# A decoder-plus-mixture kernel: expert weights in 8 KB runs, a twentieth buffer, and the overflow branch at the program's end

## The chip, the cores and the metric

The kernel runs on one core of one Trainium2 chip. The metric is the device time of one execution in microseconds (us), the median of repeated runs. Traces come from one profiled execution.

## The reference, cut to what matters

Two blocks run one after the other on 256 tokens of width 1024, all in fp32. The first block has two layers (feed-forward, retention and differential attention, feed-forward). The second block has one layer with a mixer and then a mixture of experts, and the change lies in the mixture.

```python
g_logits = h @ w_grp + b_grp                  # 4 groups
grp = argmax(g_logits)                        # one group per token
top_val, top_idx = top_k(e_logits[grp], 2)    # two of its 8 experts
gate = softmax(top_val) * p_grp
# per expert e, on the tokens that chose it:
out = (silu(xb @ w1[e]) * (xb @ w3[e])) @ w2[e]   # w1, w3: 1024x512, w2: 512x1024
y = sum of gate * out over a token's two experts
x = x + g2 * y
```

There are 32 experts. Their three matrices hold 6 MB per expert and 192 MB in all, and every one is read once from device memory.

## The kernel before, in words

The experts are worked on in 16 pairs (`pairs`, loop over `g`, NPAIR = 16). Each expert of a pair has 64 slots (CAP), so that a pair fills the 128 rows of the array's output. A pair's steps on TensorE stand in a fixed order, because every matmul of this part goes through `pin`, which keeps program order:

- `first`: 64 recorded matmuls `ph`, the tokens times w1 (bank ph0) and w3 (bank ph1), 128x64 weights against 512 columns; ScalarE puts the Silu of ph0 into `h`, VectorE multiplies ph1 in.
- `tokens(nxt)`: the gather for the next pair. For each of eight chunks k of the width, two matmuls of the normed tokens `h2` with the 0/1 matrix `pick` fill a bank `xgp`; it is scaled and shifted into `xg`, by ScalarE where k is even and by VectorE where it is odd. The banks are `tp` and `po` by turns.
- `turned`: four transposes of h into bank `ot`; `turned_out` copies one half with ScalarE, the other with VectorE into `hTe`.
- `combine(prev)`: the previous pair's weighted rows `yh` and `yl` go back to the tokens (`po` matmuls) and VectorE adds them to `xtok`. It comes in two halves of 512 columns, one ahead of each half of `last`.
- `last`: `py`, h times w2, 512 output columns at a time. After each half `weighed` makes `y` (VectorE), `yh` (ScalarE) and `yl` (VectorE).
- `slots(nxt)`: transposes and gates of the next pair, between the halves of `last`.

`route` comes before the pairs: it computes the logits, the choice of experts, each token's place in its expert and the gates.

Weights come in pieces of 1 MB into 19 places of 1 MB (`ring`), twelve pieces for a pair, all issued by SyncE's queue (SP) in order of use. A piece waits for its place, and a place becomes free when the matmuls of the piece that it held are done. Most places are memory of the mixer that ends just before (tiles such as hT, sA, xhi, raw), and the last two (e0, e1, MW = 2) belong to the mixture alone. A piece of w1 or w3 is loaded with rows k*128+p on partition p, so that its runs in device memory are one row, 512 floats or 2 KB. A piece of w2 takes half a row, 2 KB too:

```python
dma_start(w[:, k0:k1, a:b], ap[row + k0 * P:row + k1 * P, col + a:col + b]
          .rearrange("(k p) f -> p k f", p=P))
```

If an expert has more than 64 tokens, a branch (`overflow`, a `tc.If` with a loop over all pairs in it) works on the rest. With these inputs it isn't taken. It stands between pair 6 and pair 7 (OVERFLOW = 7). There the pipeline is emptied first: pair 6 is combined at once, every engine loads the largest count (`mi`) and compares and branches, and pair 7 starts after it. Pair 7's loads are issued ahead of the branch. The last pair has its pieces and its w2 product in smaller cuts, and sends each quarter of the output off as it is done.

Of the kernel before, what the change touches and what calls it, by code (L numbers as in the profile page):

```python
# [147 lines left out]
CUTS = {True: ((0, 256, 512), (0, 256, 512)), False: ((0, 512), (0, 512))}  # L148
ORD = (((0, 1, 6, 7),), ((2, 3), (4,), (5,)))
OVERFLOW = 7  # L150
MW = 2
# [15 lines left out]
def _pf_layout():  # L167
    o = 0
    for name, n in (("f1n0", 8), ("f1n1", 8), ("mxn0", 8), ("mxn1", 8), ("f2n0", 8), ("f2n1", 8),
                    ("fin", 8), ("n1w", 8), ("gn0", 4), ("gn1", 4), ("sub0", 1), ("sub1", 1),  # L170
                    ("c", 8), ("cctx", 8), ("hgw", 1), ("n2w", 8)):
# [8 lines left out]
class Kernel:  # L180
# [633 lines left out]
    def modulation(self):  # L814
# [7 lines left out]
        self.m2col = self.cp.tile([P, 2, KC], F32, name="m2col")  # L822
        self.mrow = self.dp.tile([8, 1, D], F32, name="mrow")
        for part in range(6):
# [17 lines left out]
            for i in range(1 + both):  # L842
# [17 lines left out]
                nc.scalar.dma_start(mrow, row)  # L860
                if part not in (2, 5):
                    nc.scalar.dma_start(self.mcol[:, 2 * i + part] if both else self.m2col[:, part - 3],
                                        mrow.rearrange("o (k p) -> p (o k)", p=P))
# [11 lines left out]
        nc.vector.scalar_tensor_tensor(self.rc, self.rc, 1.0, self.pf[:, o:o + KC], op0=ALU.add, op1=ALU.mult)  # L875
        cst = self.cp.tile([P, 64 + 36 + P], F32, name="cst")
# [610 lines left out]
    def pairs(self):  # L1487
# [9 lines left out]
        for g in range(NPAIR):  # L1497
            if 0 < g < OVERFLOW or g > OVERFLOW:
                ws = self.loads(g)
# [7 lines left out]
            h = self.late.tile([P, 512], F32, name="h", tag="h", bufs=1)  # L1507
            self.nc.scalar.activation(h, ph, AF.Silu)
# [3 lines left out]
            self.nc.vector.tensor_tensor(h, h, ph, op=ALU.mult)  # L1512
# [13 lines left out]
            elif g:  # L1526
                self.outputs(cur)
            if g < end:
                self.last(py, hT, ws[4], cur, 0, slice(0, 512))
                if due:  # L1530
                    self.combine(prev, due.pop(0))
                flush = g + 1 == OVERFLOW
                if not flush:
                    self.slots(nxt, self.gate_te[:, :, 2 * g + 2:2 * g + 4])
                self.last(py, hT, ws[5], cur, 1, slice(0, 512))
                prev = cur
                if flush:
                    for n in range(2):
                        self.combine(prev, slice(512 * n, 512 * n + 512))
                    ws = self.loads(g + 1)  # L1540
                    self.overflow()
                    prev = None
# [3 lines left out]
            for n in range(2):  # L1546
                for c in (slice(a, b) for a, b in zip(CUTS[True][n], CUTS[True][n][1:])):
                    self.last(py, hT, ws[4 + n], cur, n, c)
# [3 lines left out]
            self.combine(cur, due.pop(0), True)  # L1552

# [3 lines left out]


# [332 lines left out]
```

## Time and profile before

| | |
|---|---|
| median of 3 runs | 1817.65 us (1817.04 to 1818.62) |
| profiled execution, its own time | 1815.69 us |
| its span, first to last instruction | 1814.0 us |
| mean granted TensorE clock | 0.99 |
| busy share of the span: TensorE, VectorE, ScalarE, GpSimd | 97%, 57%, 41%, 19% |
| read from device memory | 424.56 MB |

The sums below are made in the span of the profiled execution; its own time is 1.7 us longer than the span and 2.0 us below the median. The experts take the last 500 us. Everything before 1300 us belongs to the first block and the mixer. DMA share is the mean busy share of the core's 16 DMA engines; packets of one engine overlap a little, so that a full load reads 1.05.

### The profile page before, as it was taken

To read this page: it belongs to the slowest core of one execution; us is meant where nothing else is said; L and a number is where in the kernel's file an instruction comes from. 1 tells how busy PE (TensorE), PEld (TensorE's weight loads), DVE (VectorE), ACT (ScalarE), POOL (GpSimd) and SP (SyncE) were. 2 spreads that over 40 slices of the span, in tenths; PEclk is the share of its full clock that TensorE was granted. 3 is DMA by queue.
4 is the path that set the end of the run, shared out by engine and by line. 5 is a ranking of instruction groups with operands and counts; after the bars stand their busy time and mean duration, and the time that the engine had idled before them with its cause. 6 is when DMAs were issued, how large, how long until landed. Compare 5 with 4: busy or idle time off the path is not lost. (4 is left out here: it accounts for less than half of the span.)

```text
span 1814.0 us, 30657 instructions
## 1 busy us (share of the span) xinstructions
PE 1757.8 (97%) x12435; PEld 1439.5 (79%) x12435; DVE 1035.4 (57%) x1764; ACT 737.1 (41%) x1312; POOL 343.8 (19%) x341
## 2 busy tenths in 40 slices
PE   9999999999999999999999999999989999899998
PEld 8999988899999999999899999986654444344444
DVE  6875887676667667668677755648332323122323
ACT  6444445454444544444455544656421111111111
POOL 3231273121221213236131102311000000000000
PEclk9999999999999999999999999999989999899999
DMA  8766643255677576754355655431789999999998
GB/s 253 231 209 192 227 163 117 70 171 166 206 232 247 174 249 211 232 189 133 114 172 170 187 190 164 160 123 41 248 315 380 397 400 400 397 400 400 399 398 306
DMA packets 312946, 427.75 MB, mean 236 GB/s; under 512 B 15056, under 2 KB 207312, under 8 KB 312672
## 3 DMA queue, kind: packets, MB, share of 16 engines
q1 hardware_dynamic: 294640, 394.51, 63.1%
q10 hardware_dynamic: 18160, 31.23, 5.2%
q8 instruction: 100, 1.64, 0.4%
q14 instruction: 46, 0.38, 0.1%
HBM read 424.56 MB, written 1.15 MB: 235 GB/s over the span
## 5 line engine op out<-in xcount | busy, mean ns | idle before, releaser
L265 DVE TENSOR_TENSOR whl<-raw,whl 128x1024 fp32r<-128x1024 f32 (+2 forms) x374 | 464.4, 1246 | 208.5 <-ACT whl L264 207.5
L264 ACT ACTIVATE whl<-raw 128x1024 fp32r<-128x1024 f32 (+2 forms) x374 | 383.8, 1032 | 331.2 <-PE pd L275 107.9
L273 PE MATMUL pgu<-xh,whl 128*128 128x272 f32 (+1 forms) x1408 | 403.8, 287 | 3.6 <-DVE g L348 3.3
L275 PE MATMUL pgu<-xh,whl 128*128 128x272 f32 (+1 forms) x1408 | 403.1, 286 | 2.4 <-DVE whl L265 2.4
L274 PE MATMUL pgu<-xl,whl 128*128 128x272 f32 (+1 forms) x1408 | 402.9, 286 | 1.4 <-DVE xl L286 1.4
L273 PEld LDWEIGHTS pgu<-xh,whl 128*128 128x128 f32 x1408 | 264.1, 188 | 5.5 <-issue 3.5
L275 PEld LDWEIGHTS pgu<-xh,whl 128*128 128x128 f32 x1408 | 265.0, 188 | 3.2 <-DVE whl L265 3.0
L274 PEld LDWEIGHTS pgu<-xl,whl 128*128 128x128 f32 x1408 | 265.1, 188 | 2.3 <-DVE xl L286 2.0
L1767 PE MATMUL ph<-ew,xg 128*64 128x512 f32 x1024 | 225.4, 597 | 6.8 <-issue 6.8
L275 PE MATMUL pd<-ah,whl 128*128 128x272 f32 (+1 forms) x704 | 203.2, 289 | 0.3 <-DVE whl L265 0.3
L274 PE MATMUL pd<-al,whl 128*128 128x272 f32 (+1 forms) x704 | 202.4, 288 | 0.0
L273 PE MATMUL pd<-ah,whl 128*128 128x272 f32 (+1 forms) x704 | 202.3, 287 | 0.0
L1767 PEld LDWEIGHTS ph<-ew,xg 128*64 128x64 f32 x1024 | 74.1, 138 | 152.0 <-issue 148.3
L352 POOL TENSOR_TENSOR u<-u,g 128x272 f32<-128x272 f32 (+1 forms) x88 | 92.1, 1047 | 397.1 <-DVE u L351 339.9
L273 PEld LDWEIGHTS pd<-ah,whl 128*128 128x128 f32 x704 | 132.9, 189 | 0.5 <-issue 0.2
L273 PE MATMUL pj<-xh,whl 128*128 128x272 f32 x448 | 133.2, 298 | 0.0
L275 PEld LDWEIGHTS pd<-ah,whl 128*128 128x128 f32 x704 | 132.5, 188 | 0.6 <-DVE whl L265 0.5
L274 PEld LDWEIGHTS pd<-al,whl 128*128 128x128 f32 x704 | 132.8, 189 | 0.1
L274 PE MATMUL pj<-xl,whl 128*128 128x272 f32 x448 | 130.5, 291 | 0.5 <-DVE xl L286 0.5
L275 PE MATMUL pj<-xh,whl 128*128 128x272 f32 x448 | 130.1, 290 | 0.0
L1787 PE MATMUL py<-ew,hTe 128*64 128x512 f32 (+1 forms) x544 | 117.4, 573 | 2.1 <-ACT hTe L1779 1.0
L1512 DVE TENSOR_TENSOR h<-h,ph 128x512 f32<-128x512 f32 x16 | 11.0, 687 | 175.6 <-PE ph L1767 175.6
(442 smaller groups left out, 2733.2 us busy)
## 6 DMA issues: line engine op xcount, KB each, us to landing
ew<-in_w_dram SPq DMA_DIRECT2D x180, 1024.0 KB, 13.8
raw<-in_ffn_w_gate_dram SPq DMA_DIRECT2D x43, 1024.0 KB, 5.5
raw<-in_ffn_w_up_dram SPq DMA_DIRECT2D x43, 1024.0 KB, 5.6
raw<-in_w_in_dram SPq DMA_DIRECT2D x38, 1024.0 KB, 5.1
raw<-in_ffn_w_down_dram SPq DMA_DIRECT2D x32, 1024.0 KB, 6.2
mraw<-in_w_mod_dram ACTq DMA_DIRECT2D x24, 1024.0 KB, 6.0
raw<-in_ffn_w_down_dram SPq DMA_DIRECT2D x16, 768.0 KB, 5.4
ew<-in_w_dram SPq DMA_DIRECT2D x24, 512.0 KB, 11.0
```

What stands on the lines that cost most here:

```text
L264: nc.scalar.activation(w[:, 0], part, AF.Copy)
L265: nc.vector.tensor_tensor(w[:, 1], part, w[:, 0].bitcast(F32), op=ALU.subtract)
L273: nc.tensor.matmul(out, wh, xh, start=first, stop=False)
L274: nc.tensor.matmul(out, wh, xl, start=False, stop=False)
L275: nc.tensor.matmul(out, wl, xh, start=False, stop=last)
L352: nc.gpsimd.tensor_tensor(u[:, :N], u[:, :N], g[:, :N], op=ALU.mult)
L1512: self.nc.vector.tensor_tensor(h, h, ph, op=ALU.mult)
L1767: self.pin(self.nc.tensor.matmul(ps[hj], cur["xg"][:, 4 * kk + k, hj], w[j][:, k], start=kk + k == 0, stop=kk == 1 and k == 3))
L1787: self.pin(self.nc.tensor.matmul(py[hj, n, c], hT[:, k, hj], w[j][:, k, c], start=k == 0, stop=k == 3))
```

## The change

- The rows of w1, w3 and w2 are dealt to the partitions in blocks: partition p holds rows 8p to 8p+7 of w1 and w3 and rows 4p to 4p+3 of w2. A piece then takes four neighbouring rows of 2 KB (w1, w3) or two neighbouring rows of 4 KB (w2), which is one run of 8 KB per partition. Pieces stay 1 MB. Only the last pair keeps smaller cuts.
- A piece of w2 is now half of its rows over all 1024 columns, not all rows over half of the columns. So `last` works through rows, and both halves of `weighed` come after its second part. The last pair uses `last_part`, which is the former order.
- The other dealing of rows is matched on the chip: h2 is written in another order of its columns, `h` is written and read with a stride of four, and scale and shift of the gather come from a second copy (`rce`, `she`), for which the mixture's modulation loads two more small rows (`m2e`).
- The gather puts odd chunks into the three rotating banks `mm` and even chunks into `tp` and `po` by turns, four or five banks where there were two.
- A twentieth place (e2, MW = 3). Its memory comes from tiles that now share or lose a buffer: `pick` and `xg` have one instead of two, `y` shares `h`, the router's small tiles share `yh`, `yl`, `hTe`.
- The branch is the last part of the program, behind the output's transfers, without the hint on which side falls through. Its own loads go to SP's queue instead of GpSimd's, and it sends the output again when it is taken. The pipeline isn't emptied between pairs 6 and 7.

```diff
@@ -145,10 +145,9 @@
 NPAIR = 16
 CAP = 64
 
-CUTS = {True: ((0, 256, 512), (0, 256, 512)), False: ((0, 512), (0, 512))}
+CUTS = ((0, 256, 512), (0, 256, 512))
 ORD = (((0, 1, 6, 7),), ((2, 3), (4,), (5,)))
-OVERFLOW = 7
-MW = 2
+MW = 3
 CONSTS = [
...
+                    nc.scalar.dma_start(self.m2e[:, part - 3], mrow.rearrange("o (p k) -> p (o k)", p=P))
...
+        self.she, self.rce = self.m2e[:, 0], self.m2e[:, 1]
+        o = PF["n2e"][0]
+        nc.vector.scalar_tensor_tensor(self.rce, self.rce, 1.0, self.pf[:, o:o + KC], op0=ALU.add, op1=ALU.mult)
...
-            if 0 < g < OVERFLOW or g > OVERFLOW:
+            if g:
...
@@ -1504,12 +1510,12 @@
             self.first(ph, cur, ws[1], 1)
             if not prev:
                 self.slots(cur, self.gate_te[:, :, 2 * g:2 * g + 2])
-            h = self.late.tile([P, 512], F32, name="h", tag="h", bufs=1)
-            self.nc.scalar.activation(h, ph, AF.Silu)
+            h = self.late.tile([P, 4, P], F32, name="h", tag="h", bufs=1)
+            self.nc.scalar.activation(self.by_row(h), ph, AF.Silu)
             ph = self.mm("ph1")
             for kk in range(2):
                 self.first(ph, cur, ws[2 + kk], kk)
-            self.nc.vector.tensor_tensor(h, h, ph, op=ALU.mult)
+            self.nc.vector.tensor_tensor(h, h, ph.rearrange("p (q k) -> p k q", k=4), op=ALU.mult)
...
             if prev:
                 cur["yh"], cur["yl"] = prev["yh"], prev["yl"]
-            elif g:
-                self.outputs(cur)
             if g < end:
-                self.last(py, hT, ws[4], cur, 0, slice(0, 512))
+                self.last(py, hT, ws[4], 0)
                 if due:
                     self.combine(prev, due.pop(0))
-                flush = g + 1 == OVERFLOW
-                if not flush:
-                    self.slots(nxt, self.gate_te[:, :, 2 * g + 2:2 * g + 4])
-                self.last(py, hT, ws[5], cur, 1, slice(0, 512))
+                self.slots(nxt, self.gate_te[:, :, 2 * g + 2:2 * g + 4])
+                self.last(py, hT, ws[5], 1)
+                for n in range(2):
+                    self.weighed(py, cur, n, slice(0, 512))
                 prev = cur
-                if flush:
-                    for n in range(2):
-                        self.combine(prev, slice(512 * n, 512 * n + 512))
-                    ws = self.loads(g + 1)
-                    self.overflow()
-                    prev = None
                 cur = nxt
                 continue
             due = []
             for n in range(2):
-                for c in (slice(a, b) for a, b in zip(CUTS[True][n], CUTS[True][n][1:])):
-                    self.last(py, hT, ws[4 + n], cur, n, c)
+                for c in (slice(a, b) for a, b in zip(CUTS[n], CUTS[n][1:])):
+                    self.last_part(py, hT, ws[4 + n], n, c)
+                    self.weighed(py, cur, n, c)
                     due.append(slice(512 * n + c.start, 512 * n + c.stop))
                     if len(due) > 1:
                         self.combine(cur, due.pop(0), True)
             self.combine(cur, due.pop(0), True)
+        self.overflow()
...
-        own, *ring = [place for place in self.ring[:-12] if place[2] == 1][-3:]
-        assert len(ring) > 1
-        with tc.If(nc.values_load(self.most[0:1, 0:1], min_val=0, max_val=SEQ) > CAP,
-                   preferred_fallthrough_block=False):
+        own, *ring = [place for place in self.ring if place[2] == 1]
+        with tc.If(nc.values_load(self.most[0:1, 0:1], min_val=0, max_val=SEQ) > CAP):
...
                         ps = self.mm("ph%d" % i)
                         for kk in range(2):
                             self.first(ps, cur, next(w), kk)
                         if i:
-                            nc.vector.tensor_tensor(h, h, ps, op=ALU.mult)
+                            nc.vector.tensor_tensor(h, h, ps.rearrange("p (q k) -> p k q", k=4), op=ALU.mult)
                         else:
-                            nc.scalar.activation(h, ps, AF.Silu)
+                            nc.scalar.activation(self.by_row(h), ps, AF.Silu)
...
-                        self.last(py, hT, next(w), cur, n, slice(0, 512))
+                        self.last(py, hT, next(w), n)
+                    for n in range(2):
+                        self.weighed(py, cur, n, slice(0, 512))
                         self.combine(cur, slice(512 * n, 512 * n + 512))
+            for tt in range(2):
+                nc.gpsimd.dma_start(A["out"][0, tt * P:(tt + 1) * P], self.xtok[:, tt])
...
-            xT = sm.tile([P, KC, P], F32, name="x2T", tag="xg", bufs=2)
+            pool, tag = ((sm, "xg"), (self.late, "yh"))[tt]
+            xT = pool.tile([P, KC, P], F32, name="x2T", tag=tag, bufs=1)
...
-            nc.scalar.activation(self.h2[:, tt], self.xtok[:, tt], AF.Copy, scale=r)
-        cnt = [0]
+            nc.scalar.activation(self.h2[:, tt].rearrange("p (k q) -> p k q", k=KC),
+                                 self.xtok[:, tt].rearrange("p (q k) -> p k q", k=KC), AF.Copy, scale=r)
+        room = self.late.tile([P, 1024], F32, name="rt", tag="yl", bufs=1)
...
-        pick = sm.tile([P, 2, P], F32, name="pick", tag="pick", bufs=2) if room is None else room[:, KC:]
+        pick = sm.tile([P, 2, P], F32, name="pick", tag="pick", bufs=1) if room is None else room[:, KC:]
...
+        xg = sm.tile([P, KC, P], F32, name="xg", tag="xg", bufs=1) if room is None else room
         return {"pick": pick, "xg": xg}
 
     def tokens(self, cur, ks):
 
         nc = self.nc
         for k in ks:
-            ps = self.pbank("xgp", ("tp", "po")[k % 2])
+            ps = self.mm("xgp") if k % 2 else self.pbank("xgp", ("tp", "po")[k // 2 % 2])
             for tt in range(2):
                 self.pin(nc.tensor.matmul(ps[:, :P], self.h2[:, tt, k * P:k * P + P], cur["pick"][:, tt],
                                           start=tt == 0, stop=tt == 1))
-            o, sc, sh = cur["xg"][:, k], self.rc[:, k:k + 1], self.sh2[:, k:k + 1]
+            o, sc, sh = cur["xg"][:, k], self.rce[:, k:k + 1], self.she[:, k:k + 1]
             if k % 2:
                 nc.vector.tensor_scalar(o, ps[:, :P], sc, sh, op0=ALU.mult, op1=ALU.add)
             else:
...
                 self.pin(self.nc.tensor.matmul(ps[hj], cur["xg"][:, 4 * kk + k, hj], w[j][:, k], start=kk + k == 0,
                                                stop=kk == 1 and k == 3))
 
+    def by_row(self, h):
+
+        return h.rearrange("p k q -> p q k")
+
     def turned(self, h):
         pt = self.pbank("hTp", "ot")
         for f in range(4):
-            self.pin(self.nc.tensor.transpose(pt[:, f * P:(f + 1) * P], h[:, f * P:(f + 1) * P], self.ident))
+            self.pin(self.nc.tensor.transpose(pt[:, f * P:(f + 1) * P], h[:, f], self.ident))
         return pt
 
     def turned_out(self, pt):
...
         self.nc.vector.tensor_copy(hT[:, 2:4], pt[:, 2:4])
         return hT
 
-    def last(self, py, hT, w, cur, n, c):
+    def last(self, py, hT, w, kk):
+
+        for k in range(2):
+            for n in range(2):
+                for j in range(2):
+                    hj = slice(CAP * j, CAP * j + CAP)
+                    self.pin(self.nc.tensor.matmul(py[hj, n], hT[:, 2 * kk + k, hj], w[j][:, k, n * 512:n * 512 + 512],
+                                                   start=2 * kk + k == 0, stop=2 * kk + k == 3))
+
+    def last_part(self, py, hT, w, n, c):
+
         for k in range(4):
             for j in range(2):
                 hj = slice(CAP * j, CAP * j + CAP)
                 self.pin(self.nc.tensor.matmul(py[hj, n, c], hT[:, k, hj], w[j][:, k, c], start=k == 0, stop=k == 3))
-        self.weighed(py, cur, n, c)
 
     def weighed(self, py, cur, n, c):
 
         nc, ns = self.nc, slice(512 * n + c.start, 512 * n + c.stop)
-        y = self.late.tile([P, 512], F32, name="y", tag="y", bufs=1)[:, :c.stop - c.start]
+        y = self.late.tile([P, 512], F32, name="y", tag="h", bufs=1)[:, :c.stop - c.start]
         yh, yl = cur["yh"][:, ns], cur["yl"][:, ns]
         nc.vector.scalar_tensor_tensor(y, py[:, n, c], cur["gs"], self.g2row[:, ns], op0=ALU.mult, op1=ALU.mult)
         nc.scalar.activation(yh, y, AF.Copy)
...
@@ -1809,27 +1827,35 @@
                 eng = nc.sync if tt else nc.scalar
                 eng.dma_start(self.A["out"][0, tt * P:(tt + 1) * P, ns], self.xtok[:, tt, ns])
 
-    def load(self, aps, ring, row, col, rows=(0, 4), cols=(0, 512), eng=None):
+    def load(self, aps, ring, rows, cols, cuts):
+
 
         ws = []
         for ap in aps:
             pool, tag, bufs = ring.pop(0)
             ring.append((pool, tag, bufs))
-            ws.append(pool.tile([P, 4, 512], F32, name="ew", tag=tag, bufs=bufs))
-        for k0, k1 in zip(rows, rows[1:]):
-            for a, b in zip(cols, cols[1:]):
-                for w, ap in zip(ws, aps):
-                    (eng or self.nc.sync).dma_start(w[:, k0:k1, a:b], ap[row + k0 * P:row + k1 * P, col + a:col + b]
-                                                    .rearrange("(k p) f -> p k f", p=P))
+            w = pool.tile([P, 4, 512], F32, name="ew", tag=tag, bufs=bufs)
+            n, f = rows.stop - rows.start, cols.stop - cols.start
+            ws.append(w.rearrange("p a b -> p (a b)").rearrange("p (a b) -> p a b", a=n, b=f))
+        for r, c in cuts:
+            for w, ap in zip(ws, aps):
+                ap = ap.rearrange("(p k) f -> p k f", p=P)
+                self.nc.sync.dma_start(w[:, r, c], ap[:, rows, cols][:, r, c])
         return ws
 
-    def weights(self, src, ring, end=False, eng=None):
-
+    def weights(self, src, ring, end=False):
+
+        every = slice(None)
         for i in range(2):
             for kk in range(2):
-                yield self.load([s[i] for s in src], ring, kk * 512, 0, (0, 2, 4) if end else (0, 4), eng=eng)
+                yield self.load([s[i] for s in src], ring, slice(4 * kk, 4 * kk + 4), slice(0, 512),
+                                [(slice(0, 2), every), (slice(2, 4), every)] if end else [(every, every)])
         for n in range(2):
-            yield self.load([s[2] for s in src], ring, 0, n * 512, cols=CUTS[end][n], eng=eng)
+            if end:
+                yield self.load([s[2] for s in src], ring, slice(0, 4), slice(512 * n, 512 * n + 512),
+                                [(every, slice(a, b)) for a, b in zip(CUTS[n], CUTS[n][1:])])
+            else:
+                yield self.load([s[2] for s in src], ring, slice(2 * n, 2 * n + 2), slice(0, D), [(every, every)])
 
 
 def body(tc, A, stop=None, skip1=False):
```

## Rows read from the trace of the kernel before

**Rows 1.** The page's slices, 40 of 45.35 us: TensorE busy, DMA share, in tenths

```profile
PE   9999999999999999999999999999989999899998
...
DMA  8766643255677576754355655431789999999998
```

**Rows 2.** Windows: length, busy us of PE, PEld, DVE, ACT, POOL; clock, DMA share, GB/s

```profile
1330.00:1340.00 10.00, 8.57 (x39) 5.86 (x40) 3.25 (x20) 0.92 (x2) 0.00 (x0) 0.71 0.40 143
1540.00:1550.00 10.00, 2.16 (x8) 1.00 (x8) 3.12 (x6) 0.63 (x1) 0.00 (x0) 0.70 1.05 390
...
1340.00:1380.00 40.00, 38.88 (x212) 16.69 (x213) 7.36 (x16) 7.54 (x16) 0.00 (x0) 1.00 0.97 352
1380.00:1790.00 410.00, 397.12 (x2082) 178.71 (x2080) 116.00 (x220) 63.13 (x140) 0.00 (x0) 0.99 1.05 398
1790.00:1802.00 12.00, 11.25 (x64) 4.95 (x62) 4.41 (x8) 0.80 (x2) 0.00 (x0) 1.00 1.02 337
```

**Rows 3.** Waits from 1380 to 1800 us: who for whom, us, times, longest

```profile
PEld xgp L1738 <- ACT xg L1744: 12.3, 42, 0.4
...
PEld ph L1767 <- DMA ew<-in_w_dram: 3.1, 11, 0.3
```

**Rows 4.** Timeline of TensorE, an ordinary pair: start us, us, instructions

```profile
1651.73 4.94 PE L1738 MATMUL xgp<-pick,h 128*128 128x128 f32 x32
1656.50 0.60 PE L1773 MATMUL hTp<-ident,h 128*128 128x128 f32 x4
...
1657.96 3.65 PE L1787 MATMUL py<-ew,hTe 128*64 128x512 f32 x16
...
1666.62 13.90 PE L1767 MATMUL ph<-ew,xg 128*64 128x512 f32 x64
...
1695.35 4.89 PE L1767 MATMUL ph<-ew,xg 128*64 128x512 f32 x22
```

**Rows 5.** Timeline of TensorE around the branch: `first` of pairs 6, 7, 8

```profile
1510.79 13.90 PE L1767 MATMUL ph<-ew,xg 128*64 128x512 f32 x64
1549.64 9.32 PE L1767 MATMUL ph<-ew,xg 128*64 128x512 f32 x32 [6.79 <-issue]
...
1580.44 4.89 PE L1767 MATMUL ph<-ew,xg 128*64 128x512 f32 x22
```

**Rows 6.** The branch's line on TensorE's sequencer: count, ns min/median/max, starts

```profile
L1561 PEldq COMPARE_BRANCH  x2: 95/3176/6257, 1542.5 to 1543.0; - x2
```

**Rows 7.** DMA view of 1133.4 to 1136.8 us, the sums load of 1 MB

```profile
DMA packets 138, 1.07 MB, mean 315 GB/s; under 512 B 4, under 2 KB 4, under 8 KB 10
```

**Rows 8.** The same load, 1135.0 to 1136.5 us: packets, then queue and share

```profile
DMA packets 76, 0.62 MB, mean 415 GB/s; under 512 B 0, under 2 KB 0, under 8 KB 0
...
q1 hardware_dynamic: 76, 0.62, 103.0%
```

**Rows 9.** DMA view, expert pieces of 2 KB: 1400 to 1422, then 1424 to 1436 us

```profile
DMA packets 4509, 8.96 MB, mean 407 GB/s; under 512 B 141, under 2 KB 141, under 8 KB 4508
...
DMA packets 2335, 4.65 MB, mean 387 GB/s; under 512 B 67, under 2 KB 67, under 8 KB 2335
```

**Rows 10.** Lines from 1220 us on: busy us, mean ns, idle before and releasers

```profile
L1744 ACT ACTIVATE xg<-xgp,m2col 128x128 f32<-128x128 f32 x64 | 29.3, 457 | 149.2 <-PE xgp L1738 145.1 <-DMA rg_dram<-place 4.1
...
L1795 DVE SCALAR_TENSOR_TENSOR y<-py,gs,g2row 128x512 f32<-128x512 f32 (+1 forms) x34 | 24.4, 719 | 76.9 <-PE py L1787 76.9
L1797 DVE TENSOR_TENSOR yl<-y,yh 128x512 fp32r<-128x512 f32 (+1 forms) x34 | 22.3, 656 | 12.0 <-ACT yh L1796 12.0
L1796 ACT ACTIVATE yh<-y 128x512 fp32r<-128x512 f32 (+1 forms) x34 | 20.6, 605 | 132.7 <-DVE y L1795 132.7
...
L1512 DVE TENSOR_TENSOR h<-h,ph 128x512 f32<-128x512 f32 x16 | 11.0, 687 | 175.6 <-PE ph L1767 175.6
```

**Rows 11.** Timeline of the last 8 us: last w2 part, last matmul

```profile
1806.15 1.95 PE L1787 MATMUL py<-ew,hTe 128*64 128x256 f32 x16
...
1810.05 0.28 PE L1805 MATMUL po<-yl,pT 128*128 128x256 f32 x1
```

More of the change, by code (lines that the diff above doesn't have):

```diff
@@ L170, in _pf_layout @@
                     ("fin", 8), ("n1w", 8), ("gn0", 4), ("gn1", 4), ("sub0", 1), ("sub1", 1),
-                    ("c", 8), ("cctx", 8), ("hgw", 1), ("n2w", 8)):
+                    ("c", 8), ("cctx", 8), ("hgw", 1), ("n2w", 8), ("n2e", 8)):
         PF[name] = (o, n)
@@ L822, in modulation @@
         self.m2col = self.cp.tile([P, 2, KC], F32, name="m2col")
+        self.m2e = self.cp.tile([P, 2, KC], F32, name="m2e")
         self.mrow = self.dp.tile([8, 1, D], F32, name="mrow")
@@ L860, in modulation @@
                 nc.scalar.dma_start(mrow, row)
+                if part in (3, 4):
+                    nc.scalar.dma_start(self.m2e[:, part - 3], mrow.rearrange("o (p k) -> p (o k)", p=P))
                 if part not in (2, 5):
@@ L1573, in overflow @@
                            for j in range(2)]
-                    w = self.weights(src, ring, eng=nc.gpsimd)
-                    h = self.late.tile([P, 512], F32, name="h", tag="h", bufs=1)
+                    w = self.weights(src, ring)
+                    h = self.late.tile([P, 4, P], F32, name="h", tag="h", bufs=1)
                     for i in range(2):
@@ L1598, in route @@
         rev = self.rev
-        before = ep.tile([P, P], F32R, name="before")
+        before = self.late.tile([P, P], F32R, name="before", tag="hTe", bufs=1)
         nc.vector.tensor_copy(before, self.before)
@@ L1635, in route @@
             r = ss[:, tt, 4:5]
-            nc.scalar.activation(self.h2[:, tt], self.xtok[:, tt], AF.Copy, scale=r)
-        cnt = [0]
+            nc.scalar.activation(self.h2[:, tt].rearrange("p (k q) -> p k q", k=KC),
+                                 self.xtok[:, tt].rearrange("p (q k) -> p k q", k=KC), AF.Copy, scale=r)
+        room = self.late.tile([P, 1024], F32, name="rt", tag="yl", bufs=1)
+        at = [0]
         def t(*dims):
-            cnt[0] += 1
-            return sm.tile([P, 2] + list(dims), F32, name="r%d" % cnt[0], tag="r%d" % cnt[0], bufs=1)
+            n = 2 * int(np.prod(dims))
+            at[0] += n
+            r = room[:, at[0] - n:at[0]]
+            return r.rearrange("p (a b c) -> p a b c", a=2, b=dims[0]) if len(dims) > 1 else r.rearrange("p (a b) -> p a b", a=2)
         tt_, pool = nc.vector.tensor_tensor, nc.gpsimd.tensor_tensor
@@ L1728, in picked @@
                                     self.iota[:, None, :].to_broadcast([P, 2, CAP]), op=ALU.is_equal)
-        xg = sm.tile([P, KC, P], F32, name="xg", tag="xg", bufs=2) if room is None else room
+        xg = sm.tile([P, KC, P], F32, name="xg", tag="xg", bufs=1) if room is None else room
         return {"pick": pick, "xg": xg}
@@ L1859, in host_arrays @@
              "hgw": np.concatenate([g["hgrn_norm_w_2"][0], g["hgrn_norm_w_2"][0]]), "n2w": g["norm2_w_2"][0]}
-    f["pf"] = np.concatenate([cols(parts[n]) for n in PF], axis=1)
+    f["pf"] = np.concatenate([cols(parts[n]) for n in PF if n != "n2e"] + [g["norm2_w_2"][0].reshape(P, KC)], axis=1)
     lv = np.stack([g["diff_lambda_q1"], g["diff_lambda_q2"], g["diff_lambda_k1"], g["diff_lambda_k2"]], axis=1)
```

## The prediction

> **What bounds the kernel now.** I read the page's slices first. From about 1270 us on, two lines stand at 9: TensorE and the DMA engines [rows 1]. Before that the DMA engines have air, so the change, which lies in the experts' part, can only matter in the last dozen slices. Both lines are candidates there and the slices can't part them.
>
> The windows say more about the DMA side. From 1380 to 1790 us the engines are full (share 1.05) at 398 GB/s [rows 2], which is 410 us x 0.398 = 163.2 MB. The reader is to see the stretch 1540 to 1550: TensorE works 2.16 of its 10 us, and the DMA engines still move 390 GB/s [rows 2]. The transfers run at their own pace whatever TensorE does; places that become free are filled at once.
>
> The timeline gives TensorE's pace. An ordinary pair goes from 1666.62 to 1695.35, 28.73 us [rows 4]. Its twelve pieces are 12.58 MB, which take 31.6 us at 398 GB/s. So TensorE eats faster than the transfers feed it, 2.9 us per pair, out of the stock in the 19 places. Around the branch it loses time: pairs 6 and 7 take 1580.44 - 1510.79 = 69.65 us where two ordinary ones take 57.46, so the emptied pipeline costs 12.2 us [rows 5]. More than half of that is one jump of TensorE's sequencer, 6.26 us [rows 6].
>
> Last the waits: between 1380 and 1800 the weight loads of `first` wait for a piece 11 times, 3.1 us in all, never over 0.3 [rows 3]. The stock lasts just to the end: pieces flow until about 1802 (share 1.02 from 1790 on) [rows 2], and the last w2 part starts at 1806.15 [rows 11]. So two chains end together, TensorE's and the transfers'. Time taken out of one alone is waited for by the other. The new end is the later of two new ends.
>
> **The transfers' chain.** *Runs of 8 KB.* The trace holds one load with packets of 8 KB, the mixer's 1 MB of sums: 76 packets with none under 8 KB move 415 GB/s at share 1.03 [rows 8]. The 2 KB pieces move 407 in one stretch and 387 in another, with the same queue and packets [rows 9]; their mean is the 398 above. I take 415 as it stands: 163.2 MB / 0.415 = 393.2 us, 16.8 less than 410. Upper bound: scaled to the share 1.05 of a full load, 415 becomes 423 and the stretch 385.8 us, 24.2 less. Lower bound: nothing, since the level of 387 comes and goes while the packets stay the same, and what makes it may not care for packet length. I take the middle value because the 8 KB row is a measurement, though of 1.5 us.
>
> By the Trainium skill, DMA: Bandwidth & Descriptors, Why small descriptors are slow (HBM only), a packet costs about three cycles beside one for each 32 bytes. As an estimate from that page, 67 cycles for the work of 64 become 259 for that of 256, 398 becomes 412 GB/s, and this term would be 13.9 us; the row's 16.8 is used.
>
> *The twentieth place.* Between 1330 and 1340 the DMA engines are busy 0.40, because all places are full and `first` of pair 0 has freed none [rows 2]. One more place takes one piece there: 1.05 MB at 398 GB/s, 2.6 us (0 if its memory comes free late). The last pair keeps small cuts, so 1790 to 1802 stays as it is. Sum: 16.8 + 2.6 = 19.4 us earlier (0 to 26.8).
>
> **TensorE's chain.** *Branch gone from the middle:* 12.2 us.
>
> *Gather.* From 1651.73 to the transposes at 1656.50 it takes 4.77 us for 32 records [rows 4]. Unhindered, the price is that of `first`: 64 half-width records of 512 columns in 13.83 us (1666.62 to the next gather, the row's 13.90 less its overlap), so 0.108 us per full-width record of 128 columns and 3.46 us for 32. That saves 1.3 us. The nearest row for what it waits for today is less: the weight loads wait 12.3 us on ScalarE's copy, 0.9 per pair over 14 pairs [rows 3]. With four or five banks a copy (0.457 us [rows 10]) has over 0.8 us until its bank is due, so I take 1.2: 15 x 1.2 = 18 us (0 to 19.5). Sum for TensorE: 30.2 us earlier (12.2 to 31.7).
>
> **Edits costed at nothing,** with their cover. The multiply into h (0.687 us [rows 10]) now reads with a stride; it runs beside the 3.5 us gather, and twice as long would still be covered. Both `weighed` after the last piece: y, yh, yl twice are 2 x (0.719 + 0.605 + 0.656) = 3.96 us [rows 10], and they must leave the buffer that y shares with h before the next Silu, which is due half of `first` later, 6.9 us. If that cover went, TensorE's chain would grow by what is over 6.9, and it has 10.8 us to spare. Single `pick` and `xg`: pick is free after `slots`, a w2 half and a whole `first` before it is needed; xg is written only after a gather that stands behind `first` on TensorE anyway. Chunk 5 of the gather takes the bank of ph1 and waits for the 0.687 us multiply, but stands 2 us behind the first chunk. `last` by rows: the same matmuls, and its first part needs only ScalarE's half of hTe. The stride in h2 and the two rows of m2e lie outside both chains' repeated part; were the cover wrong, each is paid once. On SP's queue nothing new stands ahead of a piece; the branch's own loads on SP and its two transfers on GpSimd's queue don't run.
>
> **The branch at the end.** What is queued behind it is only the program's closing. TensorE's last matmul ends at 1810.33 [rows 11], the jump of 6.26 [rows 6] would end at 1816.6 with today's clock, 2.6 us past the span's 1814.0, and the closing follows. With the DMA engines idle the jump may be shorter, and it vanishes if this side falls through. Bounds 0 to 4.5, I take 3.0.
>
> **The sum.** The later chain is that of the transfers: 19.4 - 3.0 = 16.4 us. The profiled execution's 1815.69 becomes 1799.3; it stood 2.0 us below the median, so the median becomes 1801.
>
> **Rivals.**
>
> *TensorE sets the end.* If the transfers average over 427 GB/s (163.2 MB in 410 - 27.6 us), TensorE's 30.2 count: 30.2 - 3 = 27.2, 1790. For it: 423 is near by scaling. Against it: the 387 stretches. 0.15.
>
> *The gather stays at its pace,* because copies and not banks set it. Then TensorE gains 12.2 - 3 = 9.2, and the median is 1808. For it: the wait on the copy is 0.9, not 1.3. 0.10.
>
> *Bytes bind, not packets.* Only the extra place's 2.6 counts, and the branch takes 3.0: 1818, no change. For it: one queue with one packet size has two levels, 407 and 387 [rows 9]. 0.12. [...]
>
> *Slower: the dealt rows slow the memory.* Place: the whole stretch 1380 to 1790. Neighbouring partitions now read 16 KB apart instead of one row apart. The sums load as a whole, its start included, moved 315 GB/s [rows 7]; that is the far bound and would cost over 100 us. A mild case is 380 GB/s: 163.2 / 0.380 = 429.5, 19.5 longer, less 2.6, plus 3.0: 1838. It decides from 395 GB/s down (413.2 us, 3.2 longer, so 3.6 us slower in all). Against it: the 1.5 us inside that load, at 415. 0.13. By the Trainium skill, DMA: Bandwidth & Descriptors, Latency and other measured facts, row pitches that are large powers of two lose rate, from 512 KiB on; 16 KB is below what it lists and no run here shows it. As an estimate from its smallest step, 207 of 214, 398 would become 385.
>
> **Chances.** The forecast has 0.50; its own range is 1794 to 1808 (422 to 408 GB/s). With the rivals: faster 0.50 + 0.15 + 0.10 plus a little of the third, 0.78; within 0.2% (3.6 us, about what a measurement here can tell from no change) 0.09; slower 0.13. The range 1787 to 1816 holds the forecast, the first two rivals with their bounds and part of the third, and leaves out about 2 in 10.
>
> **What would show it.** Packets of the pieces over 8 KB and the stretch from 1380 on at 408 or more: the first step. DMA share near 1 between 1330 and 1340: the place. Pairs of 27.5 us, gathers of 3.5 us, no gap between pairs 6 and 7: TensorE's chain. Then `first` of the last pairs must wait for pieces, some 10 us in sum; if it waits for none, the first rival holds. A compare-branch of some us behind the last matmul: the end. The prediction is wrong if the rate stays at 398 or falls under 395, or if pairs don't get shorter.

## The result and the profile after

The changed kernel takes 1795.69 us (median of 4 runs, 1793.32 to 1798.82), the kernel before in the same series 1818.11 (1817.04 to 1818.62): a ratio of 0.9878, 95% interval 0.9859 to 0.9898, or 22.4 us faster. The forecast was 16.4 us faster, 1801, with a range of 1787 to 1816. The profiled execution of the changed kernel took 1797.62 us, its span 1796.0.

The page's slices, TensorE and DMA share in tenths, beside [rows 1]:

```profile
PE   9999999999999999999999999998989999999998
...
DMA  8765752245576666755354565532479999999997
```

TensorE's dip in the 35th slice, where the branch stood, is gone. Windows (columns as in [rows 2]):

```profile
1330.00:1340.00 10.00, 5.70 (x23) 4.92 (x25) 4.34 (x26) 2.33 (x5) 0.00 (x0) 0.51 0.90 367
1340.00:1380.00 40.00, 39.53 (x220) 16.98 (x218) 7.44 (x16) 8.52 (x16) 0.00 (x0) 0.99 0.88 341
1380.00:1770.00 390.00, 388.87 (x2104) 178.24 (x2102) 118.91 (x222) 69.83 (x140) 0.00 (x0) 1.00 1.01 420
1540.00:1550.00 10.00, 10.00 (x55) 4.04 (x52) 0.94 (x2) 1.53 (x2) 0.00 (x0) 1.00 1.01 419
1770.00:1784.00 14.00, 13.19 (x80) 6.60 (x77) 6.14 (x13) 1.22 (x3) 0.00 (x0) 1.00 0.82 268
```

The engines move 420 GB/s instead of 398. Their share reads 1.01 where it read 1.05, and they are full all the same: packets of 2 KB read 1.05 in these traces, of 4 KB 1.03 and of 8 KB 1.01, at whatever rate they move. From 1540 to 1550 TensorE works all of the 10 us, where it worked 2.16. The two levels of [rows 9] are gone too: 5 us windows from 1380 to 1560 lie between 415 and 426. Waits from 1380 to 1800 us, against [rows 3]:

```profile
PEld xgp L1743 <- issue: 11.4, 14, 0.8
PEld ph L1772 <- DMA ew<-in_w_dram: 6.1, 12, 2.0
```

No wait of the gather for ScalarE's copy is left (12.3 us before). The waits for pieces grew from 3.1 to 6.1 us, the longest from 0.3 to 2.0. TensorE's timeline, an ordinary pair, against [rows 4]:

```profile
1645.20 13.90 PE L1772 MATMUL ph<-ew,xg 128*64 128x512 f32 x64
1659.03 3.84 PE L1743 MATMUL xgp<-pick,h 128*128 128x128 f32 x32
1662.71 0.60 PE L1782 MATMUL hTp<-ident,h 128*128 128x128 f32 x4
...
1672.81 13.90 PE L1772 MATMUL ph<-ew,xg 128*64 128x512 f32 x64
```

A pair takes 1672.81 - 1645.20 = 27.61 us (28.73 before), the gather 1662.71 - 1659.03 = 3.68 (4.77). The starts of `first` of pairs 6, 7 and 8, where [rows 5] had 69.65 us from the first to the third, are 55.24 us apart in sum:

```profile
1507.09 13.90 PE L1772 MATMUL ph<-ew,xg 128*64 128x512 f32 x64
1534.72 13.90 PE L1772 MATMUL ph<-ew,xg 128*64 128x512 f32 x64
1562.33 4.03 PE L1772 MATMUL ph<-ew,xg 128*64 128x512 f32 x18
```

The end, the timeline of all engines, against [rows 11]: `first` of the last pair is 1.2 us longer than the others, since it waits for pieces, and the last addition ends at 1789.51.

```profile
1758.55 15.09 PE L1772 MATMUL ph<-ew,xg 128*64 128x512 f32 x64
...
1788.68 0.28 PE L1823 MATMUL po<-yl,pT 128*128 128x256 f32 x1
...
1788.76 0.75 DVE L1825 TENSOR_TENSOR xtok<-xtok,po 128x256 f32<-128x256 f32 x2 [0.48 <-PE po L1823]
```

The branch's line, against [rows 6]. After the last matmul TensorE's sequencer loads the count and jumps for 4.21 us, then SP clears up. The span ends 6.5 us behind the last addition (3.1 before: 1814.0 less 1810.88):

```profile
L1558 SPq EVENT_SEMAPHORE  x8: 17/17/17, 1793.9 to 1794.4; - x8
...
L1558 PEldq TENSOR_LOAD <-mi x1: 560/560/560, 1788.3 to 1788.3; - x1
L1558 PEldq COMPARE_BRANCH  x1: 4212/4212/4212, 1789.0 to 1789.0; - x1
```

Last, a cost that the prediction had set to nothing: in the route, ScalarE's strided copies into h2 take 4.2 us (2.17 in the trace of before, both), the exponential stands behind them, and VectorE waits 1.4 us for it. First the group, then VectorE's wait between 1326 and 1336 us:

```profile
L1637 ACT ACTIVATE h<-xtok,ss 128x1024 f32<-128x1024 f32 x2 | 4.2, 2133 | 0.6 <-POOL ss L240 0.6
```

```profile
DVE rt L1694 <- ACT rt L1693: 1.4, 1, 1.4
```

The route as a whole is no longer for it. From VectorE's statistics of the tokens (`bn_stats`) to the first `first` it takes 16.6 us before (1319.49 to 1336.12) and 15.5 after (1323.78 to 1339.23). The logits are ready 2.8 us sooner: a wait of 1.2 us ahead of their first matmul is gone, and their last 16 matmuls take 1.98 us instead of 3.63 (TensorE's timeline, before, then after):

```profile
1322.77 3.63 PE L1614 MATMUL lg<-wr,x2T 128*128 128x36 f32 x16
```

```profile
1325.89 1.98 PE L1615 MATMUL lg<-wr,x2T 128*128 128x36 f32 x16 [0.25 <-ACT x2T L1613]
```

Why they were slow stays open; with the branch alone moved (e3_branch_end below) they take 3.62 us, with padding alone in the kernel before (e13_before_aligned) 1.98.

### The profile page after: what moved, and what is told of

Read it like the earlier page. It is cut to its first block, busy times and chain, and to the rows that moved or that the text cites. A ratio compares the mean times of both kernels' runs of the same rounds, so it can differ in the third digit from the quotient of the medians.

```text
span 1796.0 us, 30592 instructions
## 1 busy us (share of the span) xinstructions
PE 1749.1 (97%) x12435; PEld 1441.9 (80%) x12435; DVE 1040.9 (58%) x1765; ACT 746.6 (42%) x1312; POOL 342.5 (19%) x341
## 4 chain that ended last, share of the span: by engine, by line
## 5 line engine op out<-in xcount | busy, mean ns | idle before, releaser
L1798 PE MATMUL py<-ew,hTe 128*64 128x512 f32 x480 | 109.3, 597 | 0.5 <-ACT hTe L1788 0.5
```

Source lines behind the costliest of these rows:

```text
L1798: self.pin(self.nc.tensor.matmul(py[hj, n], hT[:, 2 * kk + k, hj], w[j][:, k, n * 512:n * 512 + 512], start=2 * kk + k == 0, stop=2 * kk + ...
```

## The experiments

The table has all kernels. "Rate" is that of the window 1380 to 1760 us in GB/s. "Waits" are those of `first` for pieces. "Experts" is the time from the start of the first `first` to the end of the last addition, "tail" from there to the end of the span, "start" the start of the first `first`, all in us of the profiled execution. Medians are set against the kernel before in the same series. Starts scatter: the six traces of the changed kernel's code up to the experts (after and e4_two_banks to e8_4k) lie between 1336.2 and 1339.2, and the two of before's (before and e3_branch_end) 3.8 us apart.

| kernel | rate | waits | start | experts | tail | median | ratio, 95% interval |
|---|---|---|---|---|---|---|---|
| before | 398 | 3.4 | 1336.1 | 474.8 | 3.1 | 1818.11 | |
| after | 420 | 6.1 | 1339.2 | 450.3 | 6.5 | 1795.69 | 0.9878 (0.9859 to 0.9898) |
| e1_rows2k | 386 | 45.4 | 1332.8 | 483.1 | 6.2 | 1825.47 | 1.0049 (1.0032 to 1.0065) |
| e2_only8k | 416 | 0.3 | 1338.2 | 475.0 | 3.0 | 1817.85 | 1.0003 (0.9993 to 1.0012) |
| e3_branch_end | 398 | 15.5 | 1339.9 | 474.6 | 5.6 | 1819.44 | 1.0009 (1.0000 to 1.0019) |
| e4_two_banks | 420 | 2.8 | 1336.4 | 462.4 | 5.8 | 1806.00 | 0.9941 (0.9924 to 0.9958) |
| e5_19places | 420 | 9.0 | 1338.4 | 452.0 | 5.9 | 1796.59 | 0.9882 (0.9866 to 0.9897) |
| e6_no_branch | 421 | 7.4 | 1337.7 | 450.8 | 2.8 | 1790.13 | 0.9852 (0.9837 to 0.9867) |
| e7_fall | 420 | 5.5 | 1336.2 | 449.7 | 8.0 | 1794.53 | 0.9880 (0.9865 to 0.9895) |
| e8_4k | 409 | 26.0 | 1337.0 | 459.7 | 6.1 | 1803.18 | 0.9922 (0.9905 to 0.9939) |
| e10_rows2k_aligned | 408 | 18.6 | 1328.0 | 459.8 | 6.2 | 1798.82 | 0.9909 (0.9894 to 0.9924) |
| e11_aligned | 425 | 3.7 | 1330.9 | 446.2 | 6.0 | 1784.76 | 0.9823 (0.9809 to 0.9836) |
| e12_aligned_h2 | 424 | 3.4 | 1329.7 | 445.3 | 5.9 | 1783.36 | 0.9820 (0.9807 to 0.9833) |
| e13_before_aligned | 407 | 3.1 | 1330.4 | 475.9 | 3.1 | 1812.09 | 0.9971 (0.9960 to 0.9982) |

**Each chain alone.** First the 8 KB runs in the kernel before: the changed kernel with MW = 2, the former gather, and OVERFLOW = 7 with the emptied pipeline. The single buffers and the later `weighed` stay.

```diff
-            ps = self.mm("xgp") if k % 2 else self.pbank("xgp", ("tp", "po")[k // 2 % 2])
+            ps = self.pbank("xgp", ("tp", "po")[k % 2])
...
+                if flush:
+                    for n in range(2):
+                        self.combine(prev, slice(512 * n, 512 * n + 512))
+                    ws = self.loads(g + 1)
+                    self.overflow()
+                    prev = None
```

> The kernel before with the 8 KB runs alone: 19 places, the gather over two banks and the branch in the middle with the pipeline emptied stay. Two chains: the rate rises to 415 to 420 GB/s, but TensorE's chain is as long as before, so no more than the 3.1 us of waits for pieces can come back, less the dearer copy on the route's path: 1813 to 1819. If the transfers alone set the end of the kernel before, 8 KB alone gives nearly the whole gain: 1797 to 1803.

Then the branch alone, in the kernel before (its hint goes and its loads move to SP's queue with it, as in the change):

```diff
-                flush = g + 1 == OVERFLOW
-                if not flush:
-                    self.slots(nxt, self.gate_te[:, :, 2 * g + 2:2 * g + 4])
+                self.slots(nxt, self.gate_te[:, :, 2 * g + 2:2 * g + 4])
...
             self.combine(cur, due.pop(0), True)
+        self.overflow()
```

> The kernel before with the branch moved to the end and the pipeline not emptied; 2 KB pieces, 19 places and the gather over two banks stay. Two chains: the transfers go on at 398 GB/s and end when they did, TensorE waits some 8 to 12 us more for pieces, and the jump behind the last matmul adds 3.4 us: 1817 to 1822. If TensorE alone sets the end of the kernel before: 12.2 less 3.4 faster, 1808 to 1811.

Neither moves the time by more than the noise. With 8 KB alone the pieces come at 416 GB/s, TensorE waits for them 0.3 us in all, and the experts take 475.0 us for 474.8: TensorE's chain has its own length (window, then waits from 1335 us on):

```profile
1380.00:1760.00 380.00, 369.34 (x1926) 165.65 (x1924) 111.08 (x208) 63.69 (x129) 0.00 (x0) 0.98 1.01 416
```

```profile
PEld ph L1782 <- DMA ew<-in_w_dram: 0.3, 1, 0.3
```

With the branch alone it is the other way round, 474.6, and the time taken out of TensorE's chain stands in the waits for pieces (the same two views):

```profile
1380.00:1760.00 380.00, 371.68 (x1944) 167.28 (x1940) 108.00 (x206) 58.78 (x130) 0.00 (x0) 1.00 1.05 398
```

```profile
PEld ph L1757 <- DMA ew<-in_w_dram: 15.5, 19, 2.5
```

So two chains end together in the kernel before, as the prediction said, and each was worth nothing alone.

**The gather's banks.** The changed kernel with the first line of the diff above alone.

> The changed kernel with the gather over the two rotating banks alone, as before. If the banks gave the gather's gain, a gather is 1.1 us longer again, a pair 28.7 us, and with 15 of them less the 6 us that TensorE waits for pieces now the time is 1804 to 1812. If the gather's gain came from something else (its place beside other work, the single buffers), a pair stays at 27.65 and the time at 1794 to 1798.

A gather goes back to 4.78 us (1668.37 to 1673.15) and a pair to 28.73:

```profile
1654.54 13.90 PE L1772 MATMUL ph<-ew,xg 128*64 128x512 f32 x64
1668.37 4.94 PE L1743 MATMUL xgp<-pick,h 128*128 128x128 f32 x32
1673.15 0.60 PE L1782 MATMUL hTp<-ident,h 128*128 128x128 f32 x4
...
1683.27 13.90 PE L1772 MATMUL ph<-ew,xg 128*64 128x512 f32 x64
```

The experts take 12.1 us more: 15 x 1.09 = 16.4 of TensorE's chain, less 3.3 of waits for pieces, leaves 13.1. The banks made the gather's gain.

**2 KB packets in the changed kernel.**

```diff
-                ap = ap.rearrange("(p k) f -> p k f", p=P)
+                ap = ap.rearrange("(k p) f -> p k f", p=P)
```

with h, h2, scale, shift, and w2's column halves as in the kernel before.

> The changed kernel with the weights dealt as before (every packet 2 KB, row f on partition f mod 128, w2 in column halves); twenty places, the new gather and the branch at the end stay. If the transfers' chain is what the 8 KB runs shortened, the stretch from 1380 us on falls back to about 398 GB/s and alternates between 387 and 407 again, TensorE waits for pieces 15 to 25 us in sum, and the time is 1808 to 1815. If bytes bind and not packets, or TensorE alone sets the end, it is 1794 to 1797.

It came out at 1825.5, above all that was expected and slower than the kernel before. The rate did not alternate; it stood at 386, and TensorE's timeline shows the pieces setting the pace:

```profile
1380.00:1760.00 380.00, 359.10 (x1886) 158.81 (x1884) 108.59 (x204) 56.87 (x126) 0.00 (x0) 1.00 1.05 386
```

```profile
1657.17 3.78 PE L1771 MATMUL ph<-ew,xg 128*64 128x512 f32 x16 [0.57 <-DMA ew<-in_w_dram]
1662.60 3.78 PE L1771 MATMUL ph<-ew,xg 128*64 128x512 f32 x16 [1.64 <-DMA ew<-in_w_dram]
```

The prediction had no account of the two levels, and here only the lower one is left. In the kernel before they come back every 50 us, and 19 places x 1.049 MB / 398 GB/s is 50.1 us: one round through the places. The addresses in the compiled programs differ in one respect:

```
start of a place within its partition, remainder by 256, in order of use
before: 224 224 | 0 0 0 0 0 0 0 0 | 224 224 224 224 224 224 | 0 | 192 192
after:   64  64 | 96 x 8          |  64  64  64  64  64  64 | 96 | 224 224 224
```

A place that starts on a multiple of 256 is called on below, any other off. The change put 64 bytes for m2e and 32 for n2e ahead of the places, and with them the nine places that were on are off too.

**Places on multiples of 256 bytes.** Padding in three pools; once in the 2 KB kernel of the last run, once in the changed kernel itself.

```diff
+        cp.tile([P, 48], F32, name="padc")
         self.wp = self.pool("wp")
...
+        pp.tile([P, 56], F32, name="padp")
         self.gp = self.pool("gp")
...
+            self.mw.tile([P, 32], F32, name="padm", tag="padm")
```

> As the run with 2 KB packets in the changed kernel (e1_rows2k, 386 GB/s flat, 1825.5 us), with 192, 224 and 128 bytes of padding in three pools, so that each of the 20 places starts on a multiple of 256 bytes within its partition; there they start at remainders of 64, 96 and 224. Theory: the level of 387 or 407 GB/s comes from where a place starts, since the kernel before had 9 of its 19 places on multiples of 256 and its rate went up and down once per round through the places. Then the rate is flat at 405 to 410 GB/s, and the time, about 0.055 x 450 = 25 us less but bounded by TensorE's chain, 1798 to 1806. Rival: the level has another cause (the rows' dealing, the phase of TensorE): the rate stays at 385 to 390 and the time at 1822 to 1828.

> The changed kernel with the same padding and nothing else: all 20 places on multiples of 256 bytes, packets of 8 KB. From three rates (2 KB at 387 beside a place that is off, 407.5 on it, 8 KB off it at 420) a packet of 8 KB takes 312.1 ns off and 4.3 ns less on a multiple, so 307.8 ns and 425 GB/s from 1380 us on. TensorE's chain sets the end with 6.1 us of waits for pieces, so 1 to 5 us are to be had: 1791 to 1795. Rival: a place's start matters by its share of bytes and not per packet, then the rate is 420 x 407.5/387 = 442 GB/s and TensorE waits for nothing. Second rival: it does not matter at 8 KB, 420 GB/s and 1793 to 1799.

Windows, first the 2 KB kernel, then the changed kernel, each with padding:

```profile
1380.00:1760.00 380.00, 372.39 (x1996) 168.86 (x1997) 114.16 (x213) 59.79 (x134) 0.00 (x0) 1.00 1.05 408
```

```profile
1380.00:1760.00 380.00, 380.00 (x2055) 171.18 (x2056) 116.05 (x217) 67.67 (x135) 0.00 (x0) 1.00 1.01 425
```

With nothing else changed, 2 KB packets go from 386 to 408 flat, and 26.7 us come back, 23.3 of them in the experts' part. At 8 KB it is 420 to 425, so a price per packet and not per byte: the median over the packet records of 1380 to 1760 us is 88 ns off and 84 on at 2 KB, 162 (e8_4k) and 159 (the last pair's pieces in e11_aligned) at 4 KB, 312 and 309 at 8 KB. By the Trainium skill, DMA: Bandwidth & Descriptors, How a descriptor splits into AXI transactions, a descriptor that doesn't start on 256 bytes has its first transaction start at the boundary below it, and the bytes that it fetches in vain cost too. The trace agrees as far as the 3 to 4 ns are about the same at all three lengths; but the page speaks of reading, and what moved here is the place that is written, so that this is the mechanism isn't shown.

Nor is the price always paid. In the changed kernel, whose places are all off, the engines are full from 1317 to 1325 us and move 427 GB/s, and 406 of the 417 packets of 8 KB take 309 ns there:

```profile
1317.00:1325.00 8.00, 7.88 (x47) 6.23 (x47) 5.60 (x9) 2.52 (x6) 2.94 (x2) 1.00 1.01 427
```

In the kernel before, the slow stretches are about one piece shorter than the runs of off places. On what else the price depends stays open. Remainders of 64, 96 and 224 are slow from 1400 us on in these runs; 128 wasn't tried.

The changed kernel with padding gains 11 us, more than the 1 to 5 expected: 4.1 lie in the experts, as expected. The rest lies ahead of them, where the padding puts the weight buffers of the first stages on multiples of 256 too. The traces start the experts 8.3 us apart, but 0.8 to 3.0 of it is that the profiled execution of the changed kernel came late (1339.2; the others with the same code up to there have 1336.2 to 1338.4).

**4 KB packets.** Each piece in two transfers.

```diff
-                                [(slice(0, 2), every), (slice(2, 4), every)] if end else [(every, every)])
+                                [(slice(0, 2), every), (slice(2, 4), every)])
```

and for w2 (slice(0, 1), every), (slice(1, 2), every).

> The changed kernel with each piece issued as two transfers whose packets are 4 KB; dealing of rows, addresses (off multiples of 256 bytes) and all else stay. From the rates so far (off: 2 KB at 387, 8 KB at 420; on: 2 KB at 408, 8 KB at 425) a packet pays about 4 ns for its bounds and 4 ns more when it starts off a multiple, so 4 KB off a multiple take 160.5 ns and the rate is 408 GB/s, with TensorE waiting 10 to 15 us more for pieces and 1799 to 1806 us. Rival: what counts is the dealing of rows (a partition's rows one behind another in memory), not the packet: 418 to 421 GB/s and 1793 to 1799.

Measured: 409 GB/s, 162 ns per packet, 26.0 us of waits (54 of up to 1.5), 1803.2. The waits are 20 us more than in the changed kernel, above the 10 to 15 expected, but the experts take only 9.4 us longer, so that not every wait is time lost. The packet's length counts, and not the dealing of rows:

```profile
1380.00:1760.00 380.00, 377.54 (x2013) 171.94 (x2010) 114.74 (x216) 67.08 (x135) 0.00 (x0) 1.00 1.03 409
```

```profile
PEld ph L1772 <- DMA ew<-in_w_dram: 26.0, 54, 1.5
```

**Padding alone in the kernel before** (8 and 56 floats in the first two pools; 17 of 19 places then lie on multiples):

> The kernel before with padding alone: 17 of its 19 places on multiples of 256 bytes (9 before), and with them the weight buffers of the first stages. Rate from 1380 us on 405 to 406 GB/s for 398. Two chains: TensorE's chain still ends when it did, so the experts' part gains no more than its 3 us of waits; the earlier stages gain what the aligned kernel showed there, 3 to 5 us: 1810 to 1815. If the transfers alone set the end: 8 us more, 1803 to 1808. If the earlier stages gain nothing: 1814 to 1818.

The rate goes to 407, and the experts take 475.9 us for 474.8: once more a faster transfer alone is worth nothing there.

```profile
1380.00:1760.00 380.00, 368.18 (x1918) 163.90 (x1920) 106.46 (x203) 57.22 (x127) 0.00 (x0) 0.99 1.05 407
```

The 5.7 us by which the experts start earlier are the whole gain. One pair of traces can't carry that, given the scatter of starts, but the medians do: 5.5 us, interval 0.9960 to 0.9982. The earlier stages run ahead of those of before by 0.9 us at 354 us and 4.3 at 805 us, and the route is 1.3 us shorter; which of their loads makes it wasn't tried.

**The twentieth place** (MW = 2 in the changed kernel):

> The changed kernel with 19 places instead of 20 (the stock of before). If the place is worth a piece's transfer while TensorE sets the end, its 2.5 us show as waits for pieces only as far as the stock runs out: 6.1 us of waits become 6 to 9, and the time is 1794 to 1799. If the place is worth its full 2.6 us: 1797 to 1799. If nothing: 1793 to 1797.

Waits for pieces are 9.0 us for 6.1, and the experts take 1.7 us longer; the medians can't tell it from nothing. What the place does can be seen at the first `first`. In the 10 us around it, 6.1 ahead and 3.9 behind, the engines move 238 GB/s with twenty places and 127 with nineteen, a difference of 1.1 MB, which is one piece:

```profile
1333.10:1343.10 10.00, 8.80 (x37) 5.86 (x37) 2.62 (x16) 0.91 (x2) 0.00 (x0) 0.63 0.59 238
```

```profile
1332.30:1342.30 10.00, 8.88 (x35) 5.96 (x37) 2.54 (x15) 0.91 (x2) 0.00 (x0) 0.60 0.32 127
```

**The branch.** Without the call of `overflow` at the end, and with the former hint:

> The changed kernel without the branch at its end (leaves out the handling of experts with more than 64 tokens, which these inputs do not need). If the branch costs what the tail grew by, the span ends about 3.1 us after the last addition instead of 6.5, and the time is 1790 to 1794. If the closing takes as long anyway: 1794 to 1798.

> The changed kernel with the branch at the end asked to be laid out as it was in the kernel before, so that the side without overflow is not the one that follows in memory by preference. If the jump behind the last matmul (4.2 us on TensorE) is the price of fetching code from far away, this layout decides whether it is paid: either 3.4 us less, 1790 to 1794, or the two jumps of the kernel before (95 ns and 6.3 us) and 1795 to 1800. If the layout changes nothing: 1793 to 1799.

Without it the tail is 2.8 for 6.5 us, so the branch costs 3.7 by this pair of traces; the other kernels with the same end have tails of 5.8 to 6.2, which makes it 3.0 to 3.7. The median is 5.6 lower, of which the rest is within the two intervals. The hint gives back the two jumps of before (95 ns and 3.9 us at the end), a tail of 8.0 and a time that can't be told apart. Neither of the two layouts makes the jump cheap.

**A better version.** The padding, and the first half of h2 by VectorE, which is idle there:

```diff
-        for tt in range(2):
-            r = ss[:, tt, 4:5]
-            nc.scalar.activation(self.h2[:, tt].rearrange("p (k q) -> p k q", k=KC),
-                                 self.xtok[:, tt].rearrange("p (q k) -> p k q", k=KC), AF.Copy, scale=r)
+        h2_, x_ = self.h2.rearrange("p t (k q) -> p t k q", k=KC), self.xtok.rearrange("p t (q k) -> p t k q", k=KC)
+        nc.vector.tensor_scalar(h2_[:, 0], x_[:, 0], ss[:, 0, 4:5], None, op0=ALU.mult)
+        nc.scalar.activation(h2_[:, 1], x_[:, 1], AF.Copy, scale=ss[:, 1, 4:5])
```

> The changed kernel with all places on multiples of 256 bytes, and the strided copy of the first 128 tokens into h2 on VectorE instead of ScalarE, where VectorE is idle waiting for the logits. If ScalarE's two strided copies (4.17 us) hold up the route by the 1.36 us that VectorE waits for the exponential, it is 1 to 1.5 us faster than the aligned kernel (1784.8): 1782.5 to 1784. If VectorE pays on the route's path what ScalarE saves: 1784 to 1786.

VectorE's copy takes 1.17 us where it waited before, ScalarE's 2.17, and the exponential comes in time (VectorE's, then ScalarE's timeline):

```profile
1318.54 1.17 DVE L1639 TENSOR_SCALAR h<-xtok,ss 128x1024 f32<-128x1024 f32 x1 [1.13 <-POOL ss L242]
```

```profile
1318.01 2.17 ACT L1640 ACTIVATE h<-xtok,ss 128x1024 f32<-128x1024 f32 x1
1320.75 0.21 ACT L1695 ACTIVATE rt<-rt 128x8 f32<-128x8 f32 x1 [0.57 <-POOL rt L1694]
```

The experts start 1.25 us earlier than in the padded kernel, while the route's statistics start at the same time in both (1315.4), and the median is 1.4 us lower, which the intervals don't separate. At 1783.4 it is the fastest of all, 12 us under the changed kernel.

## Why the prediction was right, and by how much it was off

- *Two chains.* Right, and the two runs with one chain each show it. TensorE's chain fell from 475 to about 446 us, which is the experts' time in the padded kernel, where no wait for a piece is longer than 0.3 us: 29 us, predicted 30.2.
- *Transfers end later.* Right: 450.3 us in the changed kernel, 4.1 of which the padded one recovers. The waits that were to show it are 6.1 us, predicted some 10.
- *Runs of 8 KB, 16.8 us.* The mechanism was right, the size off, and this is the term that missed. 420 GB/s instead of 415: 163.2 / 0.420 = 388.6 us, 21.4 less. The row behind 415 was a stretch of 1.5 us, and its scaling to a share of 1.05 took for granted that 8 KB packets reach that share; full, they read 1.01. The lower bound, that the level of 387 doesn't care for packet length, rested on a level I couldn't explain. It depends on where a place starts. By addresses, the change did two things at once: it took the nine good places away (398 to 386) and made packets long (386 to 420). The forecast knew of neither the 12 GB/s lost nor the 34 gained, only of a gain of 17, which is what packets of 8 KB bring where addresses are alike and on (408 to 425); that the two came out at 22 is partly luck.
- *The twentieth place, 2.6 us.* 1.7 in the experts' part by one pair of traces, not settled by time. With 21.4 it makes 24.0, and the experts' part is 24.5 shorter.
- *The gather, 1.2 us per pair.* 1.09. *The branch gone from the middle, 12.2:* pairs 6 and 7 take 55.24 us, no gap.
- *The branch at the end, 3.0.* 3.4 by the tails of before and after, 3.0 to 3.7 against the kernel without it.
- *Edits at nothing.* The cover held for the multiply into h (0.688 us, 0.687 before), single `pick` and `xg`, and both `weighed`, as the pairs' 27.61 us show. It failed for h2's stride, paid once: VectorE waits 1.4 us for it, and the route is 1.8 us longer with it than without (15.5 us for 13.7 in e1_rows2k), 1.3 in the padded kernels (15.5 for 14.2 in e10_rows2k_aligned).
- *The sum.* Experts 24.5 less, tail 3.4 more, and the route, stride and all, 1.2 less, which the prediction didn't have: 22.3. Predicted 16.4, measured 22.4 by the medians. That the two agree to 0.1 us is chance: the traces scatter by more, and between the profiled executions themselves only 18.0 us lie, because that of the changed kernel came to the route 4.3 us later.
- *The rivals.* TensorE alone setting the end became true only with padding. The gather's pace, and bytes instead of packets, fell. Slow memory through dealt rows fell: the rate rose. The one run that is clearly slower than before (e1_rows2k) is slower by addresses. By the Trainium skill, DMA: Bandwidth & Descriptors, Why small descriptors are slow (HBM only), the estimate was 398 to 412 for longer packets. On like addresses the trace has 408 to 425, that is 4.2% for the page's 3.5; off them 386 to 420.

## What to carry to other kernels

Where two chains end together, time each part alone: here 8 KB runs and the moved branch were each worth nothing, and all parts together 22 us. A rate that rises and falls with the round through the buffers can come from the buffers' addresses, as here; look at where they start before blaming or crediting anything else, because a few bytes of a new small tile can move them all. A branch moved to the end still costs its jump, here 3.0 to 3.7 us; what it saves is the emptied pipeline, here 12.2.

## What the runs showed of the hardware that was not expected

- A destination's start counts, per packet: with places off multiples of 256 bytes 2 KB packets move at 386 GB/s and on them at 408, 8 KB packets at 420 and 425. Yet for 8 us at 427 GB/s places that are off cost nothing.
- A strided copy of 128x1024 fp32 on ScalarE takes 2.1 us, an unstrided one half of that; VectorE did the strided one in 1.17.
- TensorE's jump took 3.4 to 4.3 us at the program's end. In the middle of the pairs it took 6.26 us [rows 6] and 5.9 (e13_before_aligned) beside 2 KB packets, but 3.4 beside 8 KB packets with the DMA engines 0.93 busy, so that transfers under way alone don't make it long; what does stays open. The row is that of e2_only8k:

```profile
L1569 PEldq COMPARE_BRANCH  x2: 95/1746/3397, 1547.1 to 1548.4; - x2
```
